# Two of the last expert's weight units loaded by sixteen transfers of eight partitions each

## The chip, the cores and the metric

One core of a Trainium2 chip runs the whole program. The metric is the device time of one execution in microseconds, the median of several runs; the kernel before and the changed kernel run on the same kind of core with the same inputs.

## What is computed

Two layers of a decoder trunk on 256 tokens of width 1024, in float32. The second layer ends in a mixture of experts, and that is the part that matters here:

```python
logits = xf @ router_w + router_b
top_logit, top_e = lax.top_k(logits, 2)
top_w = softmax(top_logit)
out_e = (silu(xb @ wg[e]) * (xb @ wu[e])) @ wd[e]
out[tok] += out_e * w
```

There are 8 experts. `wg[e]` and `wu[e]` are 1024 x 3584, `wd[e]` is 3584 x 1024, so the weights of one expert are 44 MB that are read from device memory (HBM) once each.

## The kernel before

All large weights are a stream of *units*, one tile `raw` of 128 partitions by at most 2048 float32 each, in the order in which the program uses them (`stream_plan`, line 76). The class `Stream` keeps that order: `fill` (line 321) lets out the load of the next unit with one `dma_start` on the SP queue (line 338), `next` hands the oldest landed unit to the work, `finish` counts it as used and calls `fill` again. The tiles come from two pools of 10 and 7 buffers, so up to 17 units can be on the way or waiting.

An expert is 46 units (`expert_units`, line 124). The inner width of 3584 is cut in four parts of 896 columns, and each part in pieces of 512 and 384 (`PIECE`). Counted from 0 within an expert:

- units 0 to 7 and 8 to 15: `wg` and `wu`, piece of 512, one unit for each 128 rows of the model width; 128 x 2048, 1024 KB each;
- units 16 to 23 and 24 to 31: `wg` and `wu`, piece of 384; 128 x 1536, 768 KB each;
- units 32 to 45: `wd`, 128 x 2048, 1024 KB each. Of the whole plan's last four units (`FINE`, line 265) each is loaded by two transfers of half the columns.

TensorE multiplies each `wg`/`wu` unit with the gathered tokens in `up` (line 1422) and each `wd` unit with the gated hidden values in `down_e` (lines 1436 and 1443). The last expert has room for 64 tokens, so a 768 KB unit is 8 matrix products, each with 32 tokens as the weights of the array and 384 columns of the unit passing through. After the last unit a short end follows: the rows are scaled (line 1583), scattered back (1588), added to `x` (1589) and stored by eight transfers (1591).

The source of an expert's units is found at run time: an expert's first unit is a number in a register of SP, and each load computes its address from it. In the program such a load stands as two rows, an `ISA` row that works on registers and the `DMA` row. Every DMA of the SP queue takes the next of eight semaphores in turn, `DMAHW0` to `DMAHW7` in the program, and waits until the DMA that had it last has landed. It also waits until TensorE has read the buffer's old unit.

Of the kernel before, what the change touches and what calls it, by code (L numbers as in the profile page):

```python
# [18 lines left out]
P = 128  # L19
# [97 lines left out]
def unit_width(u):  # L117
    return 4 * PIECE[u[4]][1] if u[0] == "gu" else UNIT
# [145 lines left out]

FINE = 4

# [25 lines left out]
class Stream:  # L295
# [25 lines left out]
    def fill(self, upto=None):  # L321
        n = min(len(self.plan) if self.offs else self.dense + (0 if self.first is None else UPE),
                self.done + self.ring if upto is None else upto)
        while self.issued < n:
            pool = self.slots.popleft()
            self.slots.append(pool)
            t = pool.tile([P, UNIT], F32, name="raw")
            name, i = self.at[self.issued]
            if name == "moe":
                at = (self.offs[i // UPE] if i >= UPE else self.first) + i % UPE  # L330
                src = self.srcs[name][bass.ds(at, 1)].rearrange("a p n -> (a p) n")
            else:
                src = self.srcs[name][i]
            w = unit_width(self.plan[self.issued])
            n = 1 if self.issued < len(self.plan) - FINE else 2
            for j in range(n):
                s = slice(j * w // n, (j + 1) * w // n)
                self.nc.sync.dma_start(t[:, s], src[:, s])
            self.raw[self.issued] = t
            self.issued += 1  # L340
# [1392 lines left out]
```

## Time and profile before

| what | value |
| --- | --- |
| median of 3 runs | 1330.96 us (1330.36 to 1330.97) |
| the profiled execution | 1328.81 us |
| its span | 1327.0 us |
| TensorE matmul busy | 1258.1 us, 95% of the span |
| VectorE, ScalarE busy | 490.9 us (37%), 304.2 us (23%) |
| moved by DMA | 472.20 MB, mean 356 GB/s |
| chain that ended last | TensorE 71%, DMA 18%, VectorE 7%, ScalarE 2% |

The span is the time from the first to the last instruction that the profiler recorded; the time of the execution holds some 2 us around it. A busy share is an average over stages with different limits, so for a change in one stage that stage's own rows are read: which wait ends last there.

### The profile page before, as it was taken

Reading aid. Unit: us, or ns where it says so; the run is one execution under the profiler, and the core shown is the slowest. Engines: PE = TensorE matmul, PEld = TensorE weight load, DVE = VectorE, ACT = ScalarE, POOL = GpSimd, SP = SyncE. Lnnn points to the kernel's source line nnn. Section 1 sums busy time; section 2 is a strip of 40 time slices with the busy share of each in tenths; the row PEclk is TensorE's granted clock in tenths of the full one; section 3 lists DMA queues with packets and bytes.
Section 4 is the critical chain, followed back from the end, with each engine's and each line's share of the span. In section 5 each row is a group of like instructions: output and inputs, shape, how many; then the busy total and the mean of one; then the engine's idle time right before and its main releaser. Section 6 shows DMA issues by size and latency. Waiting matters only on the chain.

```text
span 1327.0 us, 29821 instructions
## 1 busy us (share of the span) xinstructions
PE 1258.1 (95%) x12900; PEld 753.8 (57%) x12900; DVE 490.9 (37%) x1063; ACT 304.2 (23%) x628; POOL 1.2 (0%) x23
## 2 busy tenths in 40 slices
PE   4998999999999999999999999999979999999976
PEld 3887899999988954453224453355313354445321
DVE  8699998888868531001011000101101101100100
ACT  3175654554746432000002000002000000100000
POOL 0000000000000000000000000000000000000000
PEclk9999899999999999999999999999999999999999
DMA  9955899888410778999999999999999999999995
GB/s 381 399 214 191 357 373 377 306 343 330 182 49 12 317 284 331 408 418 415 418 419 417 417 417 416 417 417 418 416 419 419 413 417 418 406 418 417 403 418 226
DMA packets 72282, 472.20 MB, mean 356 GB/s; under 512 B 8272, under 2 KB 10320, under 8 KB 27856
## 3 DMA queue, kind: packets, MB, share of 16 engines
q1 hardware_dynamic: 72144, 470.22, 87.6%
q8 instruction: 103, 1.69, 0.5%
q14 instruction: 35, 0.29, 0.1%
HBM read 469.14 MB, written 1.05 MB: 354 GB/s over the span
## 4 chain that ended last, share of the span: by engine, by line
PE 71%; DMA 18%; DVE 7%; ACT 2%; issue 0%; DVEq 0%; SPq 0%; ACTq 0%
DMA raw<-in_moe 18%; PE acc L1422 16%; PE mm L1422 15%; PE mm L1443 8%; PE acc L1443 4%; PE mm L483 4%; PE mm L484 4%; PE mm L485 4%; PE acc L484 3%; PE acc L485 3%; PE acc L483 3%; PE mm L504 2%; DVE raw L468 1%; PE acc L521 1%; DVE cv L795 1%; PE mm L1342 1%
## 5 line engine op out<-in xcount | busy, mean ns | idle before, releaser
L1422 PE MATMUL acc<-raw,xe 128*32 128x512 f32 (+1 forms) x2688 | 259.3, 540 | 3.2 <-DMA raw<-in_moe 3.2
L1422 PE MATMUL mm<-raw,xe 128*32 128x512 f32 (+1 forms) x2688 | 258.0, 540 | 4.3 <-DMA raw<-in_moe 4.3
L1422 PEld LDWEIGHTS mm<-raw,xe 128*32 128x32 f32 x2688 | 86.3, 110 | 169.6 <-issue 153.5
L1422 PEld LDWEIGHTS acc<-raw,xe 128*32 128x32 f32 x2688 | 85.8, 110 | 164.0 <-issue 149.6
L367 ACT CAST wh<-raw 128x512 fp32r<-128x512 f32 x204 | 124.2, 622 | 114.7 <-PE mm L484 68.2
L368 DVE TENSOR_TENSOR wl<-raw,wh 128x512 fp32r<-128x512 f32 x204 | 135.7, 688 | 34.7 <-ACT wh L367 26.7
L483 PE MATMUL mm<-hh,wh 128*128 128x256 f32 x496 | 140.4, 284 | 0.5 <-ACT xr L657 0.5
L484 PE MATMUL mm<-hlo,wh 128*128 128x256 f32 x496 | 140.0, 283 | 0.3 <-DVE hlo L620 0.3
L485 PE MATMUL mm<-hh,wl 128*128 128x256 f32 x496 | 139.7, 282 | 0.0
L468 DVE SCALAR_TENSOR_TENSOR raw<-raw,crow 128x1024 f32<-128x1024 f32 x96 | 114.3, 1219 | 0.0
L1443 PE MATMUL mm<-raw,wh 128*32 128x256 f32 x2016 | 109.3, 379 | 0.0
L1558 DVE TENSOR_TENSOR wl<-wl,acc 128x512 f32<-128x512 f32 (+1 forms) x22 | 13.1, 597 | 229.1 <-PE acc L1422 229.1
L483 PEld LDWEIGHTS mm<-hh,wh 128*128 128x128 f32 x496 | 94.6, 191 | 1.7 <-issue 1.0
L484 PEld LDWEIGHTS mm<-hlo,wh 128*128 128x128 f32 x496 | 94.3, 190 | 1.1 <-issue 0.6
L485 PEld LDWEIGHTS mm<-hh,wl 128*128 128x128 f32 x496 | 94.2, 190 | 0.7 <-issue 0.7
L1443 PEld LDWEIGHTS mm<-raw,wh 128*32 128x32 f32 x2016 | 65.4, 110 | 44.0 <-issue 1.2
L1558 DVE TENSOR_TENSOR wl<-wl,mm 128x512 f32<-128x512 f32 (+1 forms) x20 | 12.0, 598 | 190.7 <-PE mm L1422 190.7
L1443 PE MATMUL acc<-raw,wh 128*32 128x256 f32 x1344 | 72.9, 379 | 0.0
L1436 PE MATMUL acc<-raw,wh 128*32 128x512 f32 x448 | 53.4, 597 | 12.1 <-DMA raw<-in_moe 12.1
L504 PE MATMUL mm<-hh,raw 128*128 128x256 f32 x256 | 60.5, 400 | 4.3 <-ACT hh L612 4.3
L1443 PEld LDWEIGHTS acc<-raw,wh 128*32 128x32 f32 x1344 | 43.7, 110 | 29.3 <-issue 0.8
L504 PEld LDWEIGHTS mm<-hh,raw 128*128 128x128 f32 x256 | 51.4, 202 | 12.8 <-ACT hh L612 5.0
(334 smaller groups left out, 1194.9 us busy)
## 6 DMA issues: line engine op xcount, KB each, us to landing
raw<-in_moe SPq DMA_DIRECT2D x236, 1024.0 KB, 19.8
raw<-in_wst SPq DMA_DIRECT2D x109, 1024.0 KB, 7.0
raw<-in_moe SPq DMA_DIRECT2D x128, 768.0 KB, 15.1
raw<-in_moe SPq DMA_DIRECT2D x8, 512.0 KB, 14.4
x<-in_xt SPq DMA_DIRECT2D x1, 1024.0 KB, 4.9
out<-x SPq DMA_DIRECT2D x8, 128.0 KB, 2.7
gw<-in_gates SPq DMA_DIRECT2D x1, 512.0 KB, 19.6
mask<-in_const SPq DMA_DIRECT2D x1, 192.0 KB, 5.1
```

Of the source, the lines that this page charges most:

```text
L367: self.nc.scalar.copy(h, t[:, j:j + PART])
L368: self.nc.vector.tensor_tensor(l, t[:, j:j + PART], h.bitcast(F32), op=OP.subtract)
L468: nc.vector.scalar_tensor_tensor(src, src, 1.0, crow, op0=OP.mult, op1=OP.mult, accum_out=raw_mod[pre][:, 2 * n + b:2 * n + b + 1])
L483: nc.tensor.matmul(o, wh, xh, start=first, stop=False, skip_group_check=skip)
L484: nc.tensor.matmul(o, wh, xl, start=False, stop=False, skip_group_check=skip)
L485: nc.tensor.matmul(o, wl, xh, start=False, stop=last, skip_group_check=skip)
L504: nc.tensor.matmul(o, wh, xh[:, k], start=(cb == 0 and k == 0), stop=(k == KB - 1), skip_group_check=True)
L521: nc.tensor.matmul(o, wh, yf[:, k], start=st, stop=sp, skip_group_check=True)
L1422: nc.tensor.matmul(ps[j * GROUP:(j + 1) * GROUP, :width], xe[:, k, r * GROUP:(r + 1) * GROUP], w[:, j * width:(j + 1) * width], start=(k = ...
L1436: nc.tensor.matmul(yb[0][t * GROUP:(t + 1) * GROUP], hs[r], w[:, f * D + h * 512:f * D + (h + 1) * 512], start=first, stop=last, skip_grou ...
L1443: nc.tensor.matmul(yb[c // 2][t * GROUP:(t + 1) * GROUP, c % 2 * 256:c % 2 * 256 + 256], hs[r], w[:, f * D + q * 256:f * D + q * 256 + 256 ...
L1558: nc.vector.tensor_tensor(h, h, ps[:, :width], op=OP.mult)
```

## The change

Two units are named by their distance from the end of the plan, 24 and 16. Counted in the last expert they are unit 22 (`wg`, rows 768 to 895 of the model width) and unit 30 (`wu`, the same rows), both of 768 KB. In place of one transfer of 128 partitions each is loaded by sixteen transfers of eight partitions by 1536 float32, 48 KB. Setting `n = 0` only skips the ordinary load below; everything else is as before.

```diff
@@ -264,6 +264,8 @@
 
 FINE = 4
 
+EIGHTS = (24, 16)
+
@@ -333,6 +335,10 @@
                 src = self.srcs[name][i]
             w = unit_width(self.plan[self.issued])
             n = 1 if self.issued < len(self.plan) - FINE else 2
+            if len(self.plan) - self.issued in EIGHTS:
+                for p in range(0, P, 8):
+                    self.nc.sync.dma_start(t[p:p + 8, :w], src[p:p + 8, :w])
+                n = 0
             for j in range(n):
                 s = slice(j * w // n, (j + 1) * w // n)
                 self.nc.sync.dma_start(t[:, s], src[:, s])
```

On the SP queue, the loads of the last expert's units 21, 22 and 23 stood like this before (`raw` is the unit's tile, `in_moe` the experts' weights in HBM, the brackets name the semaphores waited for):

```order
L338 DMA raw<-in_moe 128x1536 [waits DMAHW0_49,PE_49]
L338 ISA
L338 DMA raw<-in_moe 128x1536 [waits DMAHW1_49,PE_49]
L338 ISA
L338 DMA raw<-in_moe 128x1536 [waits DMAHW2_49,PE_49]
```

And so they stand in the changed program, where the new line is 340 and the old one 344:

```order
L344 DMA raw<-in_moe 128x1536 [waits DMAHW0_49,PE_49]
L340 ISA
L340 DMA raw<-in_moe 8x1536 [waits DMAHW1_49,PE_49]
L340 ISA
L340 DMA raw<-in_moe 8x1536 [waits DMAHW2_49]
...
L340 DMA raw<-in_moe 8x1536 [waits DMAHW0_49]
L344 ISA
L344 DMA raw<-in_moe 128x1536 [waits DMAHW1_49,PE_49]
```

Unit 22 now takes sixteen turns of the eight semaphores, each with its own pair of rows; unit 23 stands fifteen DMAs later than before. At unit 30 the rows are the same.

On TensorE, the products of units 21, 22 and 23 stood like this before:

```order
L1422 MATMUL acc<-raw,xe 32x384 [waits DMAHW0_49]
L1422 MATMUL acc<-raw,xe 32x384 x7
L1422 MATMUL acc<-raw,xe 32x384 [waits DMAHW1_49]
L1422 MATMUL acc<-raw,xe 32x384 x7
L1422 MATMUL acc<-raw,xe 32x384 [waits DMAHW2_49]
```

And now, with the line numbers moved by six:

```order
L1428 MATMUL acc<-raw,xe 32x384 [waits DMAHW0_49]
L1428 MATMUL acc<-raw,xe 32x384 x7
L1428 MATMUL acc<-raw,xe 32x384 [waits DMAHW4_49,DMAHW5_49,DMAHW3_49,DMAHW6_49,DMAHW2_49,DMAHW7_49,DMAHW1_49,DMAHW0_49]
L1428 MATMUL acc<-raw,xe 32x384 x7
L1428 MATMUL acc<-raw,xe 32x384 [waits DMAHW1_49]
```

No product moved; the first one of unit 22 waits for eight semaphores in place of one.

## Rows read from the trace of the kernel before

**Rows 1.** The chain that ended last, from 1150 us: start us, us, what

```profile
1252.56 1.02 PE acc L1422 x13
1253.58 15.01 DMA raw<-in_moe
...
1268.71 16.69 DMA raw<-in_moe
...
1285.52 19.82 DMA raw<-in_moe
...
1305.36 10.15 DMA raw<-in_moe
...
1315.55 1.11 PE acc L1436 x8
```

**Rows 2.** Busy time of the engines by stretch of the span

```profile
core 0: us, PE busy (x) PEld busy (x) DVE busy (x) ACT busy (x) POOL busy (x), PEclk, DMA share, GB/s
1200.00:1253.00 53.00, 53.00 (x707) 23.96 (x700) 7.16 (x16) 2.64 (x5) 0.00 (x0) 1.00 1.01 411
1253.00:1283.00 30.00, 23.11 (x252) 6.57 (x245) 3.09 (x6) 0.98 (x2) 0.00 (x0) 1.00 1.02 411
144.00:151.00 7.00, 4.54 (x29) 4.35 (x28) 6.10 (x17) 1.78 (x6) 0.00 (x0) 0.66 1.01 419
```

**Rows 3.** TensorE's timeline in the last expert: start us, us, instructions [idle before]

```profile
1261.07 1.50 PE L1422 MATMUL acc<-raw,xe 128*32 128x384 f32 x16 [0.39 <-DMA raw<-in_moe]
1262.97 1.50 PE L1422 MATMUL acc<-raw,xe 128*32 128x384 f32 x16 [0.40 <-DMA raw<-in_moe]
1264.86 1.50 PE L1422 MATMUL acc<-raw,xe 128*32 128x384 f32 x16 [0.39 <-DMA raw<-in_moe]
...
1278.56 1.50 PE L1422 MATMUL mm<-raw,xe 128*32 128x384 f32 x16 [0.86 <-DMA raw<-in_moe]
1280.44 1.50 PE L1422 MATMUL mm<-raw,xe 128*32 128x384 f32 x16 [0.39 <-DMA raw<-in_moe]
...
1297.92 1.92 PE L1436 MATMUL acc<-raw,wh 128*32 128x512 f32 x16 [0.58 <-DMA raw<-in_moe]
1300.41 1.92 PE L1436 MATMUL acc<-raw,wh 128*32 128x512 f32 x16 [0.57 <-DMA raw<-in_moe]
...
1311.75 1.07 PE L1436 MATMUL acc<-raw,wh 128*32 128x512 f32 x8 [0.21 <-DMA raw<-in_moe]
1313.02 1.06 PE L1436 MATMUL acc<-raw,wh 128*32 128x512 f32 x8 [0.21 <-DMA raw<-in_moe]
```

**Rows 4.** DMA issues of the whole span: xcount, KB each, median us to landing

```profile
raw<-in_moe SPq DMA_DIRECT2D x236, 1024.0 KB, 19.8
...
raw<-in_moe SPq DMA_DIRECT2D x128, 768.0 KB, 15.1
```

**Rows 5.** What the SP queue waited for, 1225 to 1320 us: total, times, longest

```profile
SPq L338 <- DMA raw<-in_moe: 61.8, 36, 2.5
```

**Rows 6.** The SP queue's timeline at 439.3 and at 1317 us

```profile
439.40 5.22 SPq L338 DMA_DIRECT2D raw<-in_moe  x9
...
1318.35 3.78 SPq L1591 DMA_DIRECT2D out<-x  x8
```

**Rows 7.** Line 338, its instructions on SP: duration ns min/median/max

```profile
L338 SPq EVENT_SEMAPHORE  x440: 17/17/14627, 34.1 to 1302.9; - x147
L338 SPq FUSED_REGOPS  x372: 42/46/66, 429.9 to 1303.3; - x186
L338 SPq MOVE raw<-in_moe x372: 29/29/37, 439.3 to 1303.4; - x186
L338 SPq DMA_DIRECT2D raw<-in_moe x372: 332/333/597, 439.4 to 1305.4; - x186
```

**Rows 8.** DMA issues between 439.3 and 439.5 us

```profile
raw<-in_moe SPq DMA_DIRECT2D x1, 1024.0 KB, 4.9
```

**Rows 9.** The DMA engines in 40 slices of 1301 to 1317 us

```profile
DMA  9789765799956999856655555555553321000000
GB/s 348 317 338 389 317 277 236 266 348 358 369 236 256 369 389 348 297 215 266 256 225 205 205 205 205 205 205 205 215 205 133 123 113 41 31 0 0 0 0 0
```

## The prediction

> **What bounds the kernel now.** Look first at the chain that ended last. From 1253.58 us on it consists almost only of pieces "DMA raw<-in_moe" of 15.01, 16.69, 19.82 and 10.15 us [rows 1]: at the end, weights arriving set the time. The busy times by stretch agree: up to 1253 us TensorE is busy 53.00 of 53 us, then only 23.11 of 30, while the DMA engines stay full at 411 GB/s [rows 2]. TensorE's timeline shows the beat. The products of a 768 KB unit take 1.50 us and start 1.89 us apart (1262.97, 1264.86), each after an idle 0.39 us that a DMA ended; units of 1024 KB come 2.49 us apart (1297.92, 1300.41), the last halves 1.27 us (1311.75, 1313.02) [rows 3]. So what delays the stream after 1253 us delays the end, unless it is caught up, and a stream that is already full catches up nothing. The two edited units lie there: unit 22 starts at 1262.97 us and unit 30 at 1278.56 us [rows 3].
>
> The stream's depth is eight transfers. A 768 KB load lands 15.1 us after its issue and a 1024 KB one 19.8 [rows 4], which is eight beats of 1.89 and of 2.49 us, and SP's own waits, 61.8 us in 36 pieces, are for a landed `raw` [rows 5]. That is the turn of the eight semaphores. Eight whole units are 15 us of work for the DMA engines; eight small ones are half a unit, under 1 us at the whole stream's pace. Here the reader should see the danger: SP must now issue quickly.
>
> **The change, step by step.**
>
> *Issues.* It adds 30 DMAs. Back to back, nine loads of line 338 take 5.22 us on SP; less the last one's 0.33 that is 4.89/8 = 0.61 us from one to the next. Eight stores without register work take (3.78-0.40)/7 = 0.48 us each [rows 6]; the 0.33 and the 0.40 are how long the last DMA instruction itself lasts, the first a median [rows 7], the second the longest store's. Of the 0.61 us, the DMA instruction is 0.33, register work 0.046, a move 0.029, a semaphore 0.017 [rows 7]. The small loads have the same rows in SP's order, so I take 0.61, and 0.48 as the low end.
>
> *The gap.* Call T0 the landing of unit 21, at 1261.07 us. The first seven small loads of unit 22 have been let out by then, one for each of the landings before; the eighth goes out at T0. Eight more follow and then unit 23, nine steps: 9 x 0.61 = 5.5 us. By then the queue is nearly empty, so unit 23 takes what a lone load takes: 4.9 us for 1024 KB [rows 8], less 2.49-1.89 for the smaller size, 4.3 us. It lands at T0+9.8. In the kernel before it landed two beats after T0, at T0+3.8 (1264.86). Lost: 6.0 us; at 0.48 a step it would be 4.3+4.3-3.8 = 4.8 us. Between the two edited units there are seven whole ones, 13.2 us of data issued in 4.3 us, so the queue is full again when unit 30 comes, and the same is lost again: **12.0 us** for both, 9.6 at the low end.
>
> *The data of the small loads.* No load in this trace goes into fewer than 128 partitions, so I bound it. If all sixteen DMA engines share each 48 KB, one takes 1.89/16 = 0.12 us and hides behind the issue. If it goes at the pace at which any eight partitions are filled now (a sixteenth of a unit, 48 KB in a beat), it takes 1.89 us. The second row is the nearer one, being about as many bytes for as many partitions; but eight neighbours need not all be one engine's share, so I halve it: 0.94 us. The first seven loads may be drained while SP waits for landings, each engine in its own time. Nine come after T0, and follow each other by 0.94 in place of 0.61 us: 9 x 0.33 = 3.0 us more for each unit, **6.0 us** for both. At 0.12 it is nothing; at 1.89 it is 9 x 1.28 = 11.5 a unit, 23 us.
>
> [...]
>
> *What costs nothing.* TensorE waits for eight semaphores before units 22 and 30; it is idle there anyway, 0.40 and 0.86 us [rows 3], and seven more at 0.017 us [rows 7] are 0.12. The last load is issued long before the eight stores, so nothing else queues behind it on SP. [...]
>
> *Sum.* 12.0 + 6.0 = 18.0 us. The profiled execution took 1328.81 us, 1.81 us more than its span of 1327.0; with the change 1346.8. The median of the runs is 2.15 us above the profiled one, so I forecast **1349.0 us**. What a measurement of this kernel can tell from no change is about 0.2%, 2.7 us.
>
> **The rivals.**
>
> *Issue alone.* Small loads spread over enough engines, or neighbouring ones overlap (two at a time bring 0.94 to 0.47 a load), so that data hides behind SP. For it: eight may be in flight, to different partitions. Against it: nothing but the nearer row above. 1330.96 + 12.0 = 1343.0 us, or 1340.6 at 0.48 a step.
>
> *Data in line.* All sixteen go one after the other, at 0.94: 15.1 in place of 1.89 us, 13.2 a unit, 26.4 for both, 1357.4 us; at 1.89 for the nine, 12.0 + 23 = 35 us, 1366 us. For it: the engines may all turn to the next small load at the same time and crowd there. Against it: seven of them are let out 1.9 us apart, before T0.
>
> *Cheap issues.* SP's 0.33 us may depend on how many rows it makes descriptors for; all its loads here have 128. At 0.2 us a step, the gap is 1.8+4.3-3.8 = 2.3 us a unit: 1335.6 us. Against it: with 512, 768 and 1024 KB alike the least is 0.332 and the median 0.333 us [rows 7], so bytes don't make it; fewer partitions would have to.
>
> *Not slower.* In the last stretch the DMA engines' busy share falls to 5 or 6 tenths and the rate to some 205 GB/s while halves still land each 1.27 us [rows 3, 9]: some engines have finished, others lag and set the beat. If eight of the sixteen carry the small loads and the laggard is among the other eight, it is spared up to 1.89 us at each edited unit, and the end comes up to 3.8 us sooner, 1327.2 us. It decides only if unit 23 is issued before the engines run dry, with nine steps in under about 2 us, a step of 0.2 us or less; against that stand 0.61 and 0.48 [rows 6].
>
> That the loads are merged again is excluded: SP's order shows all sixteen.
>
> **How the numbers follow.** Forecast (14 to 23 us more) 0.42; issue alone 0.33; data in line 0.12; cheap issues 0.08; not slower 0.05, of which 0.03 within 0.2% and 0.02 faster. The range goes from 1340 (the low end of issue alone) to 1358 us (in line at 0.94); outside are cheap issues, no loss, and the slowest line at 1.89. Slower by over 0.2%: 0.95.
>
> **What would show it.** In the changed profile: sixteen issues of 48 KB on SP about 0.6 us apart from the eighth on; most of the lost 6 to 9 us as one wait of TensorE before unit 22, the rest before unit 23, and the same before units 30 and 31; before 1261 us nothing moved; after 1285 us the old beats, 2.49 and 1.27 us, all later by the same amount. If the DMA engines are idle within the gap, issue set it; if eight or fewer work through it, the data did. Wrong would be: steps under 0.3 us, one unit late and not the other, or a beat that is longer to the end.

## The result and the profile after

The changed kernel takes **1348.74 us** (median of 4 runs, 1347.65 to 1349.03), the kernel before beside it 1330.93 us. The ratio is 1.0133, 95% interval 1.0122 to 1.0145: 17.8 us slower. The forecast was 1349.0.

| | before | after |
| --- | --- | --- |
| the profiled execution | 1328.81 us | 1348.5 us |
| its span | 1327.0 us | 1346.7 us |
| mean rate of DMA | 356 GB/s | 351 GB/s |
| DMA share of the chain that ended last | 18% | 30% |

Where the 19.7 us between the two spans lie is read from TensorE's timeline of the changed kernel, in the last expert (line 1428 is 1422 of before, 1442 is 1436):

```profile
1264.95 1.50 PE L1428 MATMUL acc<-raw,xe 128*32 128x384 f32 x16 [0.75 <-DMA raw<-in_moe]
1271.64 4.93 PE L1428 MATMUL acc<-raw,xe 128*32 128x384 f32 x32 [5.19 <-DMA raw<-in_moe]
1276.78 1.50 PE L1428 MATMUL mm<-raw,xe 128*32 128x384 f32 x16 [0.21 <-DMA raw<-in_moe]
...
1287.16 1.50 PE L1428 MATMUL mm<-raw,xe 128*32 128x384 f32 x16 [0.90 <-DMA raw<-in_moe]
1293.80 4.10 PE L1428 MATMUL mm<-raw,xe 128*32 128x384 f32 x32 [5.14 <-DMA raw<-in_moe]
1298.69 1.92 PE L1442 MATMUL acc<-raw,wh 128*32 128x512 f32 x16 [0.80 <-DVE wh L1420]
...
1312.40 1.93 PE L1442 MATMUL acc<-raw,wh 128*32 128x512 f32 x16 [1.87 <-DMA raw<-in_moe]
...
1332.69 1.07 PE L1442 MATMUL acc<-raw,wh 128*32 128x512 f32 x8 [0.29 <-DMA raw<-in_moe]
```

Unit 21 starts at 1264.95, unit 22 only at 1271.64, after a wait of 5.19 us; unit 29 starts at 1287.16 and unit 30 at 1293.80, after 5.14. Before, those waits were 0.40 and 0.86 us [rows 3]. From the first product of unit 16 to that of the last half unit it takes 77.0 us in place of 63.2 (1255.68 to 1332.69, and 1252.38 to 1315.55 before): **13.8 us are lost in the last expert**. 3.3 us are there before unit 16, and 2.5 us come after the last store.

The chain that ended last (start us, us, what) names what the waits are made of:

```profile
1247.54 17.37 DMA raw<-in_moe
1264.93 0.28 SPq L340
...
1269.12 0.28 SPq L340
...
1273.17 13.95 DMA raw<-in_moe
1287.13 0.28 SPq L340
...
1290.95 0.28 SPq L340
...
1301.28 21.08 DMA raw<-in_moe
1322.37 10.27 DMA raw<-in_moe
```

Where there were only DMA pieces [rows 1], two runs of SP's own issuing stand between them. SP's timeline, merged, shows nine small loads from the eighth of each unit on:

```profile
1264.93 4.47 SPq L340 DMA_DIRECT2D raw<-in_moe  x9
```
```profile
1287.13 4.09 SPq L340 DMA_DIRECT2D raw<-in_moe  x9
```

Less the last one's 0.28, the first row is 4.19/8 = 0.52 us a step and the second 3.81/8 = 0.48. And the DMA engines meanwhile (the first two columns after the stretch are its length and TensorE's busy time, the last three the granted clock, DMA share, GB/s):

```profile
1264.00:1270.00 6.00, 1.70 (x20) 0.42 (x16) 0.00 (x0) 0.00 (x0) 0.00 (x0) 0.93 0.25 74
1270.00:1276.00 6.00, 4.36 (x28) 1.26 (x32) 0.00 (x0) 0.23 (x1) 0.00 (x0) 0.50 0.94 282
```
```profile
1288.00:1291.00 3.00, 0.66 (x11) 0.00 (x0) 0.00 (x0) 0.00 (x0) 0.00 (x0) 1.00 0.51 119
```

At the first gap they are a quarter busy; at the second half busy, at 119 GB/s, which is 48 KB in 0.41 us. From the issue of the last small load to TensorE's next product it is 2.52 us at the first gap (1269.12 to 1271.64) and 2.85 at the second (1290.95 to 1293.80), so where the engines are twice as busy the last load comes only 0.3 us later behind its issue.

### The profile page after: what moved, and what is told of

Its sections match the earlier page's. It is cut to its first block, busy times and chain, and to the rows that moved or that the text cites. A ratio compares the mean times of both kernels' runs of the same rounds, so it can differ in the third digit from the quotient of the medians.

```text
span 1346.7 us, 29919 instructions
## 1 busy us (share of the span) xinstructions
PE 1264.6 (94%) x12900; PEld 758.4 (56%) x12900; DVE 491.1 (36%) x1063; ACT 303.6 (23%) x628; POOL 1.2 (0%) x23
## 4 chain that ended last, share of the span: by engine, by line
PE 60%; DMA 30%; DVE 6%; ACT 1%; SPq 1%; issue 1%; DVEq 0%; ACTq 0%
DMA raw<-in_moe 30%; PE acc L1428 12%; PE mm L1428 11%; PE mm L1449 5%; PE mm L489 4%; PE mm L491 4%; PE mm L490 4%; PE acc L491 3%; PE acc L490 3%; PE acc L489 3%; PE acc L1449 3%; PE mm L510 2%; DVE raw L474 1%; PE acc L527 1%; DVE cv L801 1%; PE mm L1348 1%
```

## The experiments

All changes are to the changed kernel's loop over small loads, or to its list of units. "Unit 16 to last" is the time between the two starts named above; "end" counts from the start of the first store's issue to the end of the span. Ratios are to the kernel before, on the same chip.

| run | loads for each edited unit | ratio [95%] | unit 16 to last, us | end, us |
| --- | --- | --- | --- | --- |
| before | 1 of 128 partitions | 1 | 63.2 | 8.7 |
| c0 | the same, again | | 62.7 | 8.7 |
| the change | 16 of 8 | 1.0133 [1.0122, 1.0145] | 77.0 | 11.2 |
| e1 | 16 of 8, unit 22 only | 1.0082 [1.0065, 1.0099] | 71.0 | 10.2 |
| e2 | 16 of 8, four apart | 1.0157 [1.0140, 1.0175] | 82.0 | 10.8 |
| e3 | 16 of 128 by 96 columns | 1.0130 [1.0106, 1.0154] | 77.0 | 11.0 |
| e4 | 8 of 16 | 1.0084 [1.0060, 1.0109] | 72.2 | 10.1 |
| e10 | 8 of 128 by 192 columns | 1.0048 [1.0031, 1.0065] | 67.9 | 9.3 |
| e5 | 4 of 32 | 1.0086 [1.0069, 1.0103] | 73.9 | 9.0 |
| e7 | 4 of 32, four apart | 1.0009 [0.9999, 1.0019] | 62.8 | 8.9 |
| e8 | 4 of 128 by 384 columns | 1.0007 [0.9997, 1.0016] | 62.8 | 8.7 |
| e9 | 2 of 64 | 1.0092 [1.0075, 1.0109] | 73.6 | 8.7 |
| e6 | 16 of 8, three experts earlier | 1.0113 [1.0095, 1.0132] | 62.4 | 10.9 |

**c0: the kernel before, a second profile.** Expected:

> The kernel before, profiled a second time, as a control. In the first pair of profiles the changed kernel is later by 19.7 us at the end of the span: 3.3 us are there already at unit 16 of the last expert, 13.8 us come between the first product of unit 16 and that of the last unit (63.2 us before, 77.0 us with the change), and 2.5 us come after the last store's issue (4.9 us before, 7.4 us with the change). Theory 'chance ahead': the 3.3 us ahead of the last expert are the spread between two executions, and this profile shows its first product of unit 16 anywhere between 1252 and 1256 us, with 63 us from there to the last unit again. Theory 'caused ahead': it is at 1252.4 us again, within 0.3 us. The end after the last store stays 4.9 us by either.

Measured: TensorE's timeline has unit 16 at 1254.60 us, 2.2 us later than in the first profile.

```profile
1254.60 2.76 PE L1422 MATMUL acc<-raw,xe 128*32 128x384 f32 x32
```

So most of the 3.3 us ahead of the last expert can be the spread between executions; in the other runs unit 16 starts between 1252.77 and 1255.73 (e6 aside).

**e1: only unit 22.**

```diff
-EIGHTS = (24, 16)
+EIGHTS = (24,)
```

> Only unit 22 in sixteen transfers. Theory 'issue' (the nine issues that stand on SP after the landing of the unit ahead, and the time of a lone load, make the gap; data hides): from the first product of unit 16 to that of the last unit 63.2 + 5 to 7 us, unit 30 without a gap. Theory 'data' (the prediction's: nine small loads follow each other by 0.94 us): 63.2 + 9 us. Theory 'SP program length' for the 2.5 us after the last store: with 30 rows more on SP in place of 60 the end is either 4.9 or 7.4 us and nothing in between, since it is one fetch of instructions more or not. Total against before: issue 5 to 9 us, data 9 to 12.

Measured: 71.0 us, 7.9 more than before; unit 22 waits 5.21 us and unit 30 only 1.68. More than half of the 13.8 is lost at the first unit. It lies between what the two theories expected and decides little. After the last store the end is 5.0 us, near the 4.9 of before, but issuing the eight stores takes 5.23 us in place of 3.78 (SP's timelines), so that the whole end, 10.2 us, lies between 8.7 and 11.2: "nothing in between" was wrong.

**e2: eight partitions that are four apart.**

```diff
-                for p in range(0, P, 8):
-                    self.nc.sync.dma_start(t[p:p + 8, :w], src[p:p + 8, :w])
+                for p in [32 * g + r for g in range(4) for r in range(4)]:
+                    self.nc.sync.dma_start(t[p:p + 29:4, :w], src[p:p + 29:4, :w])
```

> Sixteen transfers of eight partitions for each of the two units, as in the change, but the eight are four partitions apart in place of neighbours. The number of issues is the same. Theory 'issue': the same time as the changed kernel within 1.5 us (unit 16 to last unit 75 to 78 us). Theory 'data' (neighbours share a narrow way into the memory): eight partitions spread out are quicker, and 6 us are gained, 69 to 72 us. Beside it, the rate while DMA engines work on small loads alone, 113 GB/s in the changed kernel at half busy share: by 'crowding of neighbours' the busy share falls towards a quarter, since a row of 6 KB then takes 0.24 us as in a whole load; by 'a row alone is slow' it stays at half.

Measured: 82.0 us, slower than the change, which neither theory expected. SP's timeline and the busy times of the second gap tell why:

```profile
1287.62 7.47 SPq L340 DMA_DIRECT2D raw<-in_moe  x9
```
```profile
1288.00:1294.00 6.00, 1.15 (x16) 0.26 (x8) 0.00 (x0) 0.00 (x0) 0.00 (x0) 0.84 0.18 55
```

An issue of this form lasts 0.645 us (the median of line 340 in e2's profile) and a step (7.47-0.645)/8 = 0.85. The data got cheaper for the DMA engines: a busy share of 0.18 at 55 GB/s is 0.0033 for each GB/s, against 0.51/119 = 0.0043 for neighbours and 1.02/411 = 0.0025 for whole units [rows 2]. Yet the time grew by 4.9 us, near the 18 steps that grew by 0.37 us (6.7). The time followed the issues, not the data; most of what is missing to 6.7 lies ahead of the edited units, see below.

**e3: sixteen loads of 96 columns.**

```diff
+                for p in range(0, w, w // 16):
+                    self.nc.sync.dma_start(t[:, p:p + w // 16], src[:, p:p + w // 16])
```

> Sixteen transfers for each of the two units, of all 128 partitions by 96 columns. The number of issues and the bytes of each are the same, partitions and DMA engines are all in use. Theory 'issue': 17 us more than before again, within 2 us (unit 16 to last unit 75 to 79 us; a little more where SP takes 0.33 in place of 0.28 us for an issue, nine of them a unit are 0.9 us for both). Theory 'data': the partitions were what made it slow, so 6 us less than the changed kernel, 69 to 72 us.

Measured: 77.0 us, the same as the change. With all partitions in use nothing is gained, so for sixteen loads the data is not what sets most of the loss. SP's nine loads at the second unit take (4.94-0.33)/8 = 0.58 us a step:

```profile
1284.41 4.94 SPq L340 DMA_DIRECT2D raw<-in_moe  x9
```

Counted from the eighth small load, units 23 and 31 leave SP after 5.22 and 5.20 us here, after 4.73 and 4.35 in the change (SP's timelines): 1.3 us more, and still the loss is the same. What made up for it is seen ahead of the edited units. From unit 16 to 21 and from 26 to 29 (TensorE's timelines) the change takes 9.3 and 6.2 us, before 8.7 and 5.7, e2 8.1 and 5.7, e3 8.2 and 5.8: where the small loads don't lie on neighbouring partitions, the stretches ahead of the gaps are some 1.6 us shorter than in the change. With that, e2 should be 6.7 - 1.6 = 5.1 us slower than the change (4.9 measured), and e3 within 0.3 us of it (0.0 measured).

**e4: eight loads of sixteen partitions.**

```diff
-                for p in range(0, P, 8):
-                    self.nc.sync.dma_start(t[p:p + 8, :w], src[p:p + 8, :w])
+                for p in range(0, P, 16):
+                    self.nc.sync.dma_start(t[p:p + 16, :w], src[p:p + 16, :w])
```

> Eight transfers of sixteen partitions, 96 KB each, for each of the two units. Theory 'issue': only one small load is still to go out when the unit ahead lands, unit 23 one step behind it; 0.5 + 0.5 + 4.3 us (a lone load) in place of 3.8, so 1 to 2.5 us a unit with a slow restart, 2 to 5 us in all against before (unit 16 to last unit 65 to 68 us, 62.7 and 63.2 in the two profiles of before). Theory 'data' by the prediction's pace (0.94 us for each load, now of twice the partitions and bytes): 8 x 0.94 in place of 1.89, 5.6 us a unit, 11 us in all, 74 us. End after the last store, by program length (28 rows more on SP): 5.3 to 6.4 us.

Measured: 72.2 us, between the two. The end is 10.1 us, of which issuing the stores is 5.08.

**e5: four loads of 32 partitions.**

```diff
-                for p in range(0, P, 8):
-                    self.nc.sync.dma_start(t[p:p + 8, :w], src[p:p + 8, :w])
+                for p in range(0, P, 32):
+                    self.nc.sync.dma_start(t[p:p + 32, :w], src[p:p + 32, :w])
```

> Four transfers of 32 partitions, 192 KB each, for each of the two units. Theory 'issue': when the unit ahead lands, all four small loads and four whole units are already out, so the engines never run dry: 0 to 1 us in all, within 0.2% of before. Theory 'data': 4 x 0.94 in place of 1.89 us, 1.9 us a unit, 3.8 us in all, 66.5 us from unit 16 to the last unit.

Measured: 73.9 us. Both theories fell: four issues cost SP nothing, and still 10.7 us are lost, three times what the data theory allowed. TensorE's timeline of e5 shows it at whole units, 27 to 29, ahead of the edited one:

```profile
1279.26 2.48 PE L1428 MATMUL mm<-raw,xe 128*32 128x384 f32 x16 [2.07 <-DMA raw<-in_moe]
1282.83 2.79 PE L1428 MATMUL mm<-raw,xe 128*32 128x384 f32 x16 [1.10 <-DMA raw<-in_moe]
1286.31 2.79 PE L1428 MATMUL mm<-raw,xe 128*32 128x384 f32 x16 [0.69 <-DMA raw<-in_moe]
```

They come 3.5 us apart in place of 1.89, and the DMA engines are as busy as can be at little more than half the rate:

```profile
1276.00:1288.00 12.00, 8.14 (x60) 1.99 (x56) 0.00 (x0) 0.00 (x0) 0.00 (x0) 0.65 1.03 232
```

**e7, e8, e9: the same bytes, other partitions.** e7 takes 32 partitions four apart, e8 all 128 by 384 columns, e9 64 neighbours. The new loop of e7, of e8 and of e9:

```diff
+                for p in range(4):
+                    self.nc.sync.dma_start(t[p:p + 125:4, :w], src[p:p + 125:4, :w])
```
```diff
+                for p in range(0, w, w // 4):
+                    self.nc.sync.dma_start(t[:, p:p + w // 4], src[:, p:p + w // 4])
```
```diff
+                for p in range(0, P, 64):
+                    self.nc.sync.dma_start(t[p:p + 64, :w], src[p:p + 64, :w])
```

> Four transfers of 192 KB for each of the two units as in the run with four of 32 neighbours, but the 32 partitions are four apart and lie all over the 128. That run lost 10.9 us between unit 16 and the last unit although four issues are nothing for SP, and its DMA engines were 99% busy at 205 to 280 GB/s, half the usual rate, for some 12 us. Theory 'crowding' (32 neighbours are half of the ways into the memory, and rows of whole units that lag behind crowd there too): with the partitions spread the rate stays near 400 GB/s and nothing is lost, 63 to 65 us from unit 16 to the last unit, 0 to 2 us against before. Rival 'depth' (a small load holds one of eight turns, so fewer bytes are in flight and the engines that are ahead run dry): the same loss, 72 to 75 us.

> Four transfers of 192 KB for each of the two units, of all 128 partitions by 384 columns. By 'crowding' no loss, 63 to 65 us from unit 16 to the last unit; by 'depth' 72 to 75 us. Where this one and the spread partitions differ, the row size (1.5 KB here, 6 KB there) made it.

> Two transfers of 64 neighbouring partitions, 384 KB, for each of the two units. 'Crowding' with half of the ways for 64 neighbours as for 32: the rate falls to some 209 GB/s while engines work on them, and the loss is like that of four of 32, 7 to 12 us in all. 'Crowding' with ways in proportion to partitions: as for 128 partitions by half, three quarters or more of the rate, a loss of 3 us or less. 'Depth': two turns in place of one, 2 us or less.

Measured: e7 and e8 lose nothing (62.8 us both, ratios of 1.0009 and 1.0007), e9 loses as much as e5. Busy times of e7, then of e9, over 12 us around the whole units between the edited ones:

```profile
1269.00:1281.00 12.00, 9.20 (x100) 2.58 (x96) 0.00 (x0) 0.61 (x2) 0.00 (x0) 1.00 1.02 416
```
```profile
1276.00:1288.00 12.00, 7.30 (x64) 1.85 (x64) 0.00 (x0) 0.00 (x0) 0.00 (x0) 0.86 1.03 277
```

416 GB/s against 277, with all engines busy. "Depth" is excluded: e5 and e7 hold the same turns with the same bytes. That the partitions are neighbours is the cause; by which way inside the chip, no run shows. 64 neighbours cost as much as 32: e9 loses 10.4 us and e5 10.7, and both are well below the 417 GB/s that the kernel before moves from 1276 to 1288 us (277 and 232 GB/s). The rate of eight neighbours by themselves is shown by no run here: the changed kernel moved 119 GB/s in the second gap, with several small loads to different partitions in flight.

**e10: eight loads of 192 columns**, to part the two causes at eight.

```diff
+                for p in range(0, w, w // 8):
+                    self.nc.sync.dma_start(t[:, p:p + w // 8], src[:, p:p + w // 8])
```

> Eight transfers of 96 KB for each of the two units, of all 128 partitions by 192 columns: as many issues as in the run with eight of sixteen neighbours, which lost 9.2 us between unit 16 and the last unit, without neighbours to crowd. 'Issue' alone, worked out for eight (one small load still to go out when the unit ahead lands): 65 to 68 us from unit 16 to the last unit, so that 'crowding' made the rest of those 9.2 us. If instead it is 71 to 73 us again, crowding has no part at eight and the issue costs more than was worked out. End after the last store 6.4 us, as in the other runs with about 30 rows more on SP.

Measured: 67.9 us against e4's 72.2. By that difference, of e4's 9.0 us over before some 4.8 are issue and restart and 4.2 crowding. The end was expected as in e1 and e4, with as many rows, and is 0.8 to 0.9 us shorter (9.3 us).

**e6: the units of an earlier expert.**

```diff
-EIGHTS = (24, 16)
+EIGHTS = (24 + 3 * 46, 16 + 3 * 46)
```

> The same sixteen transfers of eight partitions at units 22 and 30, but of the expert three before the last, where TensorE is as good as never idle. Theory 'a full stream catches up nothing': the DMA engines are full from there to the end, so the loss of some 13 us comes through whole, 12 to 16 us against before at the end, with the last expert itself as before (63 us from unit 16 to the last unit). Rival 'cover': landed units are in stock there and TensorE sets the pace, so the stream finds time again, under 8 us. Theory 'SP program length': 60 rows more on SP, so the end after the last store is 7.4 to 7.9 us as in the changed kernel although the last expert's loads are untouched; if the small loads themselves made it, 5.3.

Measured: ratio 1.0113, 14.5 us, with the last expert itself as before (62.4 us). The loss came through: TensorE starts the next expert 14.0 us later than before (1011.06 for 997.09) and unit 16 of the last one 14.0 us later too (1266.37 for 1252.38). In between both kernels keep TensorE busy all the time and the DMA engines at a share of 1.01, so that neither had time to spare; which of the two alone would have been enough is not shown. The end is 10.9 us although no load of the last expert is touched. What SP waited for there, in e6, then in the change, then before:

```profile
SPq L1698 <- SPq L1698: 4.8, 2, 2.6
```
```profile
SPq L1698 <- SPq L1698: 5.0, 2, 2.7
```
```profile
SPq L1692 <- SPq L1692: 2.5, 1, 2.5
```

## Why the prediction was right, and which steps of it were not

The time, 1348.74 us, is the forecast's 1349.0, but not by the forecast's terms.

- **Bound and place: right.** The stream sets the end; nothing was caught up (in e6 not over three experts either); two gaps at units 22 and 30, most of each before the unit itself.
- **The gap by issues: right in kind, at its low end in size.** The prediction took 0.61 us a step and named 0.48 as the low end; the steps are 0.52 at the first unit and 0.48 at the second. The 0.61 was a mean over uneven steps: the nine loads of [rows 6] start at 439.40, 439.96, 440.50, 441.02, 441.87, 442.40, 442.92, 443.45 and 444.29 us (SP's timeline), six steps of 0.52 to 0.56 and two of 0.85. A load of eight neighbours holds SP 0.28 us, not 0.33, so "cheap issues" was right in direction, by 0.05 us. Unit 23 went out 4.73 us after the eighth small load (1264.93 to 1269.66, SP's timeline) and unit 31 4.35 us (1287.13 to 1291.48), in place of 5.5; with the prediction's 4.3 for a lone load and 3.8 for before the term is 5.2 + 4.9 = 10.1 us, not 12.0. That the time follows SP is shown by e2, where a longer issue of cheaper data cost 4.9 us more, and by e3, where all partitions gained nothing.
- **The data of the small loads: wrong.** This is the step that failed: "the second row is the nearer one ... so I halve it: 0.94 us", 6.0 us in the sum. The measured pace in the second gap is 0.41 us a load, less than SP's step, so it hid but for the 0.3 us above. By the prediction's own sign, engines that work through the gap, the second gap would have been put down to the data: they are half busy all through it, and yet the last load came only that little behind its issue. The rival "issue alone" had the mechanism of the gap. What neighbours do cost in the change lies where the prediction had nothing, ahead of the gaps, where small loads are drained beside whole units: 1.1 us of the 13.8 (0.6 from unit 16 to 21, 0.5 from 26 to 29), or 1.6 against e2 and e3.
- **What made up for it** the prediction did not name. Of the 13.8 us in the last expert, the waits at units 22 and 30 give 9.1 (5.19-0.40 and 5.14-0.86). 0.6 are lost before unit 21, where small loads already stand among whole ones. From unit 22 to 26 it takes 9.3 us in place of 7.6 (TensorE's timelines), so the restart after the first gap cost 1.8. 1.4 come after unit 33, nearly all of it in unit 37's wait of 1.87 us, which is 0.57 for its neighbours; 1.0 is spread between units 26 and 33. And 2.5 us come after the last store.
- **TensorE's clock fell, and the loss was covered.** TensorE stood still for 5.19 us before 1271.64; the granted clock was 0.50 from 1270 to 1276 us; units 22 and 23 took 4.93 us together, where one such unit took 1.50 before [rows 3]. Unit 24 still waited 0.21 us for its DMA, so the loss by the clock was covered.
- **The sum was right by cancellation.** 12.0 + 6.0 was forecast. The issue term by the measured steps is 10.1; the other 3.7 us of the last expert and the 2.5 at the end, 6.2 together, came from what the prediction did not name or had elsewhere, and that this is near its 6.0 for the data is luck. The profiles show 13.8 + 2.5 = 16.3, and the medians 17.8; the rest is within what two executions differ by ahead of the last expert (2.2 us between the two profiles of before).

## What to carry to other kernels

When a stream is full and a fixed number of transfers may be in flight, as here, splitting a transfer costs what the issuing queue needs between the last landing ahead and the next large load, and that load's own time on an empty queue: count the issues that stand there and multiply by the step of that form of issue, which the trace has; look at the single steps and not only at their mean. Where a split is wanted, cut columns or spread the partitions: four pieces of either kind were free here, four or two of neighbouring partitions cost 11 us. And a sum that comes out right is no proof of its terms; the run that changes one term alone (e7 for the partitions; nearly so e3 for the data) is.

## What the runs showed of the hardware that was not expected

- **Two or four loads of neighbouring partitions cost more than sixteen cost by crowding** (10.4 and 10.7 us in e9 and e5, 1.1 to 1.6 in the change), and the loss falls on whole units ahead of them: 3.5 us a beat in e5 at 232 GB/s with all engines busy. That engines which are ahead fill the ways that the laggards still need is argued from this, not shown. Two edited units at half pace would be 2 x 1.89 = 3.8 us; that it was 10.7 stays open.
- **The form of a load sets how long SP needs to issue it**: 0.28 us for eight neighbouring partitions, 0.32 for 16 or 32 and 0.50 for 64 (medians of line 340 in the change, e4, e5 and e9), 0.33 for 128, 0.47 for 32 that are four apart (e7), 0.645 for eight that are four apart (e2). Fewer partitions are not always the cheaper issue.
- **The end from the first store on grows with SP's program**: 8.7 us for up to 4 rows more, 8.7 to 9.0 for 12 (e8, e7, e5), 9.3 to 10.2 for 28 to 30 (e10, e4, e1), 10.8 to 11.2 for 60 (e2, e6, e3, the change). With 28 to 30 the extra lies in the issuing of the stores, 4.27 to 5.23 us in place of 3.78, with 60 behind it, where SP waits for itself twice in place of once. What it waits for was not tried.
- **After a gap one small disturbance may be enough.** In the stretch before unit 37's late start, 1308 to 1314 us, the changed kernel's DMA queues have one packet of the queue that the profile calls instruction:

```profile
q8 instruction: 1, 0.02, 1.1%
```

1.1% of 16 engines over 6 us is 1.1 us on one engine, about what unit 37 was late. The kernel before has such a packet in the last expert too, between 1293 and 1299 us, and no unit is late behind it: there some DMA engines had a lead of several us [rows 9] on which such a packet may fall unseen, while after a gap all may start level. This is an inference from the traces of the change, e2, e3, e4 and e10, in all of which unit 37 waits 1.7 to 2.0 us and such a packet falls in the few us ahead; no run tested it.
